# The shared expert of a mixture of experts computed behind the ninth expert unit instead of around the router

## The chip, the cores and the metric

One NeuronCore of a Trainium2 chip runs the whole program in one launch. The metric is device time in microseconds of one execution. Before the change three runs took 1607.09, 1607.56 and 1607.63 us; the median is 1607.56 us. A separate execution with the hardware profiler took 1610.33 us.

## The reference, cut to what matters

The program is two transformer blocks on 256 tokens of width 1024, all weights in fp32. The first block ends in a mixture of experts with 64 routed experts, 8 per token, and one shared expert that every token passes:

```python
def swiglu(x, wg, wu, wd):
    return (jax.nn.silu(x @ wg) * (x @ wu)) @ wd

h2 = modulate(rms_norm(x, norm_ffn_g), sh_ffn, sc_ffn)        # 256 x 1024
scores = jax.nn.sigmoid(h2 @ w_router)                        # 256 x 64
_, idx = lax.top_k(scores + b_router, 8)
wts = scores at idx, divided by their sum, times 2.5
routed[t] = sum over e in idx[t] of swiglu(h2[t], w_e_gate[e], w_e_up[e], w_e_down[e]) * wts[t, e]
y = swiglu(h2, w_sh_gate, w_sh_up, w_sh_down) + routed        # shared: 1024 -> 256 -> 1024
out = x + g_ffn * y
```

## The kernel before, in words

**Stages.** Most of the first block (input projection, attention, gating, output projection) runs until about 336 us of the profile. Then come the router (`routing`, called from `block1`), the mixture of experts (`moe`, until about 828 us) and the second block.

**Weights.** All weights are fetched by one stream of 1 MB transfers on SyncE's queue, in an order fixed when the kernel is built (`Ring`, line 222). During the experts there are 17 slots of 1 MB. `done` releases a slot and at once issues the next transfer of the list into it; SyncE works the list strictly in order. Each routed expert has three such chunks: two halves of gate and up, one of down. The shared expert has gate (`i_sh[0]`), up (`i_sh[1]`) and down (`i_sh[2]`). Before the change, gate and up stand in the list directly ahead of the first expert, and down behind unit 10 (`SH_DOWN`).

**Router stage.** For each half of the tokens (t = 0, 1) `x1_fm(t)` transposes the normalised tokens into `h2` (features in partitions), `logits(t)` multiplies them with the router's weights, `top(t)` selects eight on VectorE, `position()` counts with a few small matmuls, and `mkS(0)` builds the 0/1 matrix `S` that picks the tokens of the first units. The 32 matmuls of the shared expert's gate and up for t = 0 are put between these (`more`): one behind each router matmul, 4 behind the second transposes, 7 ahead of `position` and 5 behind it. `follow()` holds TensorE to that order.

**Experts.** The experts are taken in 26 units (`UNITS`) of one, two or four experts that share the 128 columns of the array, in 13 groups g of two units. For group g+1, `mkS` builds `S` and `gather` multiplies it with the normalised tokens (`xnh`, `xnl`, the high and low parts) to `xg`, 128 x 8 x 256, two quarters of it in each unit of group g. In unit p, `gu` multiplies `xg` with gate and up (in fp32, each expert in its own column group of the array), `act` applies silu and the product, `tra` transposes, `down` multiplies with the down weights, one unit late, and `comb` adds the rows into four accumulators, two units late. `trS` makes the matrix for `comb`.

The 32 shared matmuls for t = 1 are in unit 0, behind `trS` and ahead of its gathers; the shared down product (`shared_down`, 8 matmuls) is behind unit 10. Its result goes into the same accumulators.

**Order.** Source order is a priority only. When the kernel is built, a scheduler writes the order of each engine's instructions from the times at which it expects operands to be there. On the chip each engine runs its own list in order.

Of the kernel before, what the change touches and what calls it, by code (L numbers as in the profile page):

```python
# [9 lines left out]
F32 = mybir.dt.float32  # L10
F32R = mybir.dt.float32r
# [3 lines left out]
OP = mybir.AluOpType  # L15
# [256 lines left out]
class Kernel:  # L272
# [295 lines left out]
    def program(self):  # L568
        tc, nc, A = self.tc, self.nc, self.A
        with ExitStack() as es:  # L570
# [33 lines left out]
            for n in range(15, 33):  # L604
# [2 lines left out]
                self.i_ada += put([ada[j] for j in aorder[len(self.i_ada):len(self.i_ada) + na]], False)  # L607
            self.i_ga, self.i_gb, self.i_upa, self.i_upb, self.i_out = (
                ids[0:4], ids[4:8], ids[8:12], ids[12:14], ids[14:18])
            self.i_sh = put(w1[33:35], False)  # L610
            self.i_e, self.i_d = [], []
            self.of_rank = {}

            def chunk(r, j):
# [6 lines left out]
            for p, (n, r) in enumerate(UNITS):  # L621
                self.i_e.append(put([chunk(r + e, j) for j in range(2) for e in range(n)], False))
                if p:
                    self.i_d.append(downs(p - 1))
                if p == self.SH_DOWN:
                    self.i_sh += put(w1[35:36], False)
            self.i_d.append(downs(len(UNITS) - 1))
            self.i_2 = [put(w2[l * N_W2:(l + 1) * N_W2], True) for l in range(2)]
# [16 lines left out]
    R0 = 3  # L645
    HI = 2

    SH_DOWN = 10
    ADA_ORDER = (0, 1, 3, 4, 2, 5)
    ADA_AFTER = {8: 1, 10: 2, 11: 2, 12: 1, 13: 2, 14: 1, 15: 1, 16: 1, 17: 1, 18: 1, 19: 1, 20: 1, 21: 1}  # L650

# [130 lines left out]
    def block1(self):  # L782
# [353 lines left out]
        with self.follow():  # L1136
            x1_fm(0)
        x1_split(0)

        sh = iter(self.shared(h2, 0, self.mmp))  # L1140

        def more(n):
            for _ in range(n):
                next(sh)()

        for t in range(2):
            for f in logits(t):
                with self.follow():
                    f()
                    more(1)  # L1150
            if t == 0:
                with self.follow():
                    x1_fm(1)
                ends = [self.last(e) for e in (mybir.EngineType.Activation, mybir.EngineType.DVE)]
                with self.follow():
                    more(4)
        after = self.sigmoid
        with tc.issue_after(ends[0]), tc.issue_after(ends[1]):
            x1_split(1)
            top(0)  # L1160
        top(1)
        with self.follow():
            more(7)
        with self.follow():
            position()
        with self.follow():
            more(5)
        self.dump("h2", h2[:])
        adap_es.close()
        self.moe(xnh, xnl, gf, h2, after, mmes, ranks, overflow)  # L1170
        ext3_es.close()
        ext2_es.close()
        xp2_es.close()
# [355 lines left out]

        return pool.tile([128, 512], F32, tag="bank", name=name, bufs=3)  # L1530

    def shared(self, h2, t, pool):

        nc = self.nc
        ps = self.bank(pool, "shy") if t else pool.tile([128, 512], F32, tag="mm", name="shy")
        self.shp = ps

        def step(n, m, k):
            w = self.ring.get(self.i_sh[n])[:].rearrange("p (k c) -> p k c", k=8)
            j = 2 * n + m  # L1540
            nc.tensor.matmul(ps[:, j * 128:(j + 1) * 128], w[:, k, m * 128:(m + 1) * 128], h2[:, t, k],
                             start=j == 0 and k == 0, stop=j == 3 and k == 7, skip_group_check=True)
            if t and m and k == 7:
                self.ring.done(self.i_sh[n])

        return [lambda n=n, m=m, k=k: step(n, m, k) for n in range(2) for m in range(2) for k in range(8)]

    def shared_act(self, t):
        nc = self.nc
        if t == 0:  # L1550
            self.sgt = self.xp.tile([128, 2, 256], F32, tag="x01", name="sgt")
        ps = self.shp[:].rearrange("p (n m c) -> p n m c", n=2, m=2)
        o = self.sgt[:, :, t * 128:(t + 1) * 128]
        nc.scalar.activation(o, ps[:, 0], AF.Silu)
        nc.vector.tensor_tensor(o, o, ps[:, 1], op=OP.mult)

    def moe(self, xnh, xnl, gf, h2, after, mmes, ranks, overflow):
        tc, nc, A, c, sm = self.tc, self.nc, self.A, self.c, self.sm
        extp = self.extp
        mp, mp_es = self.pool("moe")  # L1560
# [4 lines left out]
        st = {}  # L1565
        nu = len(UNITS)
        xgs = [self.hip.tile([128, 8, 256], F32, tag="hl", name="xg")]
        wx = []
        for _ in range(2):
            t = self.hip.tile([128, SLOT], F32, tag="hl", name="wx")  # L1570
# [13 lines left out]
        def mkS(g):  # L1584
            S = mp.tile([128, 2, 2, 128], F32R, tag="S", name="S")
            for u in (2 * g, 2 * g + 1):
                n, _ = UNITS[u]
                for t in range(2):
                    i = nc.vector.tensor_tensor(unit(S, u)[:, t], io1[:, None, 0:128 // n].to_broadcast([128, n, 128 // n]),
                                                table(u, 0)[:, t], op=OP.is_equal)  # L1590
            st["S", g] = S
            return i

        def mkW(g):
            W = self.xp.tile([128, 2, 2, 128], F32, tag="x00", name="SW")
# [3 lines left out]

        def gather(g, q):  # L1600
            S = st["S", g]
            xg = xgs[g % 2]
            ps = self.bank(pg)
            for kk in range(2):
                k = 2 * q + kk
                o = ps[:, kk * 256:(kk + 1) * 256]
                n = 0
                for t in range(2):
                    for src in (xnh[:], xl):
                        nc.tensor.matmul(o, src[:, t, k * 128:(k + 1) * 128], S[:, t].rearrange("p u s -> p (u s)"),  # L1610
                                         start=kk == 0 and n == 0, stop=n == 3, skip_group_check=True)
                        n += 1
            for kk in range(2):
                k = 2 * q + kk
                i = ps[:, kk * 256:(kk + 1) * 256]
                if kk:
                    nc.vector.tensor_scalar(xg[:, k], i, self.a2[:, k:k + 1], self.mod[:, 3, k, 0:1], op0=OP.mult, op1=OP.add)
                else:
                    nc.scalar.activation(xg[:, k], i, AF.Identity, scale=self.a2[:, k:k + 1], bias=self.mod[:, 3, k, 0:1])

        def gu(p, k):
            if k == 0:
                st["gu"] = pg.tile([128, 512], F32, tag="gu", name="gu")
            xg = xgs[p // 2 % 2]
            n = UNITS[p][0]
            m = 128 // n
            ids = self.i_e[p][k // 4 * n:k // 4 * n + n]
            for e, i in enumerate(ids):
                s0 = (p % 2) * 128 + e * m
                w = self.ring.get(i)[:].rearrange("p (k c) -> p k c", k=4)  # L1630
                nc.tensor.matmul(st["gu"][m * e:m * e + m, :], xg[:, k, s0:s0 + m], w[:, k % 4, :], start=k == 0, stop=k == 7,  # L1631
                                 tile_position=(0, m * e))
            if k % 4 == 3:
                for i in ids:
                    self.ring.done(i)
# [41 lines left out]
        def comb(p):  # L1677
            ST = st.pop(("ST", p))[0]
            for h in range(2):
                yh, yl = st.pop(("y", p, h))  # L1680
                for t in range(2):
                    for y in (yh, yl):
                        nc.tensor.matmul(self.acc[t][h][:], ST[:, t * 128:(t + 1) * 128], y[:],
                                         start=False, stop=False, skip_group_check=True)

        def shared_down():
            i = self.i_sh[2]
            w = self.ring.get(i)[:].rearrange("p (k c) -> p k c", k=2)

            for k in range(2):  # L1690
                nc.vector.tensor_tensor(w[:, k], w[:, k], gf[:], op=OP.mult)
            for t in range(2):
                for h in range(2):
                    for k in range(2):
                        nc.tensor.matmul(self.acc[t][h][:], self.sgt[:, k, t * 128:(t + 1) * 128], w[:, k, h * 512:(h + 1) * 512],
                                         start=False, stop=False, skip_group_check=True)
            self.ring.done(i)

        i = mkS(0)
        ranks(None, -1)  # L1700
        with tc.issue_after(after.ins), tc.issue_after(i.ins):
            self.shared_act(0)
        mmes.close()
        pg = es.enter_context(tc.tile_pool(name="pg", bufs=1, space=PSUM))
        for q in range(5):
            if q < 4:
# [5 lines left out]
        for p in range(nu):  # L1712
            g = p // 2 + 1
            more = 2 * g < nu
            if p % 2 == 0 and more:
                mkS(g)

            for k in range(8):
                if p:
                    gu(p, k)  # L1720
                if k == 3:
                    if p > 1:
                        comb(p - 2)
                    trS(p)
                    if p == 0:
                        for f in self.shared(h2, 1, pg):
                            f()
                        self.shared_act(1)
                        xgs.append(self.hip.tile([128, 8, 256], F32, tag="hl", name="xg"))
                    if more:  # L1730
                        for q in range(2):
                            gather(g, 2 * (p % 2) + q)
                if p == 0 and k in (4, 7):
                    ranks(pg, int(k == 7))
            act(p)
            if p:
                down(p - 1, 0)
                down(p - 1, 1)
            tra(p)
            if p % 2 and more:  # L1740
                mkW(g)
            if p == 1:
                overflow(pg)
            if p == self.SH_DOWN:
                shared_down()
        self.fg = []
        for h in range(2):
# [657 lines left out]
```

## Time and profile before

| | |
|---|---|
| median of three runs | 1607.56 us |
| profiled execution | 1610.33 us, of which the span of the trace 1608.5 us |
| TensorE matmul (PE) busy | 1558.0 us (97%) |
| TensorE weight load (PEld) busy | 1204.3 us (75%) |
| VectorE / ScalarE busy | 874.2 us (54%) / 632.7 us (39%) |
| read from memory | 413.05 MB, 259 GB/s over the span |
| costliest group of the experts | L1631 `gu`, 936 records, 206.8 us |

Busy time of PE is the union of matmul records, whose ends are modelled. Each fp32 matmul leaves two records; some records are missing. The profile cuts the span in 40 slices of 40.2 us: the experts fill slices 10 to 21. L numbers are lines of the kernel before.

### The profile page before, as it was taken

What the parts mean: (1) busy time and instruction counts of PE and PEld (TensorE: products, weight loads), DVE (VectorE), ACT (ScalarE), POOL (GpSimd) and SP (SyncE); (2) the same over time, 40 slices, a digit from 0 to 9 for tenths busy, and PEclk for the clock granted to TensorE, in tenths of its full rate; (3) what the DMA queues carried; (4) which work ended last, traced back from release to release, by engine and by line L of the source; (5) the groups of instructions that cost most, each with busy time, mean ns of one, the idle gap of its engine ahead of it and who ended that gap; (6) DMA issues with size and microseconds to landing.
All of it is one profiled execution on the core that took longest, in us unless ns stands there. A gap on an engine that the chain in (4) does not pass through costs nothing. (4 is left out here: it accounts for less than half of the span.)

```text
span 1608.5 us, 26028 instructions
## 1 busy us (share of the span) xinstructions
PE 1558.0 (97%) x10509; PEld 1204.3 (75%) x10509; DVE 874.2 (54%) x1647; ACT 632.7 (39%) x1171; POOL 12.8 (1%) x23
## 2 busy tenths in 40 slices
PE   6999998999999999999989999999999999999997
PEld 4799876975444444444349999899999999899996
DVE  3696597663332323332354667864446566975454
ACT  3633376441111111111134656454433656544440
POOL 0000000000000000000000000000000000000000
PEclk9999899999999999999999999999999999999999
DMA  9789676879999999999965446565552444655530
GB/s 363 275 307 292 194 204 210 307 288 347 403 421 421 420 420 421 420 421 420 422 241 186 146 147 212 187 239 185 186 178 81 156 158 143 244 216 210 184 131 27
DMA packets 62973, 419.48 MB, mean 261 GB/s; under 512 B 7394, under 2 KB 9058, under 8 KB 14211
## 3 DMA queue, kind: packets, MB, share of 16 engines
q1 hardware_dynamic: 59010, 408.63, 67.6%
q0 software_dynamic: 1088, 5.61, 1.1%
q10 hardware_dynamic: 2752, 3.55, 0.6%
q8 instruction: 83, 1.36, 0.3%
q14 instruction: 40, 0.32, 0.1%
HBM read 413.05 MB, written 4.19 MB: 259 GB/s over the span
## 5 line engine op out<-in xcount | busy, mean ns | idle before, releaser
L353 DVE TENSOR_TENSOR wlo<-w,whi 128x1024 fp32r<-128x1024 f32 (+1 forms) x384 | 375.3, 1016 | 182.3 <-ACT whi L352 179.5
L352 ACT CAST whi<-w 128x1024 fp32r<-128x1024 f32 (+1 forms) x384 | 319.3, 883 | 317.2 <-PE mm L393 144.3
L392 PE MATMUL mm<-xTh,whi 128*128 128x256 f32 x960 | 274.5, 286 | 0.0
L394 PE MATMUL mm<-xTh,wlo 128*128 128x256 f32 x960 | 271.5, 283 | 0.0
L393 PE MATMUL mm<-xTl,whi 128*128 128x256 f32 x960 | 271.0, 282 | 0.0
L1631 PE MATMUL gu<-w,xg 128*64 128x512 f32 (+2 forms) x936 | 206.8, 596 | 0.0
L392 PEld LDWEIGHTS mm<-xTh,whi 128*128 128x128 f32 x960 | 182.9, 191 | 2.2 <-issue 1.4
L393 PEld LDWEIGHTS mm<-xTl,whi 128*128 128x128 f32 x960 | 183.4, 191 | 0.6
L394 PEld LDWEIGHTS mm<-xTh,wlo 128*128 128x128 f32 x960 | 182.8, 190 | 0.0
L1631 PEld LDWEIGHTS gu<-w,xg 128*64 128x64 f32 (+2 forms) x936 | 59.2, 127 | 99.4 <-issue 94.9
L1670 PE MATMUL y<-w,aT 128*64 128x512 f32 (+2 forms) x432 | 114.4, 599 | 0.0
L1768 ACT CAST yh<-yf 128x512 fp32r<-128x512 f32 x52 | 32.2, 619 | 126.1 <-DVE yf L1767 124.4
L1652 DVE SCALAR_TENSOR_TENSOR sil<-sil,wsl,gu 128x256 f32<-128x256 f32 x26 | 12.5, 481 | 126.6 <-ACT sil L1651 126.0
L1767 DVE TENSOR_TENSOR yf<-y,gf 128x512 f32<-128x512 f32 x52 | 35.9, 690 | 79.3 <-PE y L1670 79.3
L392 PE MATMUL mm<-hh,whi 128*128 128x256 f32 x256 | 74.4, 293 | 3.4 <-ACT whi L352 1.8
L394 PE MATMUL mm<-hh,wlo 128*128 128x256 f32 x256 | 74.9, 294 | 1.2 <-DVE wlo L353 1.0
L1670 PEld LDWEIGHTS y<-w,aT 128*64 128x64 f32 (+2 forms) x432 | 32.7, 126 | 57.5 <-issue 56.0
L393 PE MATMUL mm<-hl,whi 128*128 128x256 f32 x256 | 74.4, 292 | 0.5 <-DVE hl L289 0.5
L484 PE MATMUL acc<-whi,xTh 128*128 128x256 f32 x256 | 74.0, 290 | 0.0
L485 PE MATMUL acc<-wlo,xTh 128*128 128x256 f32 x256 | 72.8, 285 | 0.0
L486 PE MATMUL acc<-whi,xTl 128*128 128x256 f32 x256 | 72.6, 287 | 0.1
L1651 ACT ACTIVATE sil<-gu 128x256 f32<-128x256 f32 x26 | 10.0, 384 | 132.7 <-PE gu L1631 132.7
(450 smaller groups left out, 3119.3 us busy)
## 6 DMA issues: line engine op xcount, KB each, us to landing
w<-in_we SPq DMA_DIRECT2D x171, 1024.0 KB, 19.8
w<-in_w SPq DMA_DIRECT2D x156, 1024.0 KB, 4.9
w<-in_wada SPq DMA_DIRECT2D x23, 1024.0 KB, 9.8
wx<-in_we SPq DMA_DIRECT2D x21, 1024.0 KB, 19.8
ks<-kd SPq DMA_DIRECT2D x8, 512.0 KB, 8.1
lngb<-in_rows POOLq DMA_DIRECT2D x4, 1024.0 KB, 5.7
T<-in_rpb SPq DMA_DIRECT2D x8, 384.0 KB, 8.9
qs<-qd SPq DMA_DIRECT2D x16, 128.0 KB, 7.7
```

The costliest lines, as they stand in the source:

```text
L352: nc.scalar.copy(hi[:, s], w[:, s])
L353: self.lo_of[i] = nc.vector.tensor_tensor(lo[:, s], w[:, s], hi[:, s].bitcast(F32), op=OP.subtract)
L392: nc.tensor.matmul(ps, hi[:, k, mm], h, start=first, stop=False, skip_group_check=True)
L393: nc.tensor.matmul(ps, hi[:, k, mm], l, start=False, stop=False, skip_group_check=True)
L394: nc.tensor.matmul(ps, lo[:, k, mm], h, start=False, stop=last, skip_group_check=True)
L484: nc.tensor.matmul(o, h, wh, start=k == 0 and c % 2 == 0, stop=False, skip_group_check=True)
L485: nc.tensor.matmul(o, h, wl, start=False, stop=False, skip_group_check=True)
L486: nc.tensor.matmul(o, l, wh, start=False, stop=k == 7 and c % 2 == 1, skip_group_check=True)
L1631: nc.tensor.matmul(st["gu"][m * e:m * e + m, :], xg[:, k, s0:s0 + m], w[:, k % 4, :], start=k == 0, stop=k == 7, tile_position=(0, m * e))
L1670: nc.tensor.matmul(y[m * e:m * e + m, :], st["aT"][:, f * 128 + e * m:f * 128 + e * m + m], w[:, f, h * 512:(h + 1) * 512], start=f == 0, ...
L1767: nc.vector.tensor_tensor(t[0:n], y[0:n], g[0:n, h * 512:(h + 1) * 512], op=OP.mult)
L1768: nc.scalar.copy(yh[0:n], t[0:n])
```

## The change

Gate and up of the shared expert leave the head of the list of transfers and are put behind unit 9; shared down moves from behind unit 10 to behind unit 11. No shared matmul is left in the router stage or in unit 0. An extra group is put between groups 4 and 5: `mkI` builds an identity in place of `S`, and the usual `gather` with it, in units 8 and 9, gives `xg` for all 256 tokens. Group 5's own `mkS` and `gather` move from units 8 and 9 to behind unit 9, where each quarter of the gather follows one of four calls of `shared`, of 8 matmuls each, now 256 columns wide for both token halves at once. The second `xg` buffer is taken before the loop instead of inside unit 0.

```diff
-            self.i_sh = put(w1[33:35], False)
-                if p == self.SH_DOWN:
+                if p == self.P_SH:                    # P_SH = 9
+                    self.i_sh += put(w1[33:35], False)
+                if p == self.P_SH + 2:
                     self.i_sh += put(w1[35:36], False)
...
             for f in logits(t):
                 with self.follow():
                     f()
-                    more(1)
...
+        def mkI():
+            S = mp.tile([128, 2, 2, 128], F32R, tag="S", name="S")
+            for t in range(2):
+                o = S[:, t].rearrange("p u s -> p (u s)")
+                for h in range(2):
+                    i = o[:, h * 128:(h + 1) * 128]
+                    if h == t:
+                        nc.vector.tensor_copy(i, self.ident)
+                    else:
+                        nc.vector.tensor_scalar(i, self.ident, 0.0, None, op0=OP.mult)
...
+        def shared(n, m):
+            i = self.i_sh[n]
+            w = self.ring.get(i)[:].rearrange("p (k c) -> p k c", k=8)
+            if m == 0:
+                st["sh"] = self.bank(pg, "shy")
+            ps = st["sh"]
+            for k in range(8):
+                nc.tensor.matmul(ps[:, m * 256:(m + 1) * 256], w[:, k, m * 128:(m + 1) * 128], st["xg", "all"][:, k],
+                                 start=m == 0 and k == 0, stop=m == 1 and k == 7, skip_group_check=True)
+            if m:
+                f = sgt[:].rearrange("p a b -> p (a b)")
+                if n == 0:
+                    nc.scalar.activation(f, ps[:], AF.Silu)
+                else:
+                    nc.vector.tensor_tensor(f, f, ps[:], op=OP.mult)
+                self.ring.done(i)
...
             if p % 2 == 0 and more:
-                mkS(g)
+                mkI() if sh else mkS(g)               # sh: the group behind unit 9
...
-                    if p == 0:
-                        for f in self.shared(h2, 1, pg):
-                            f()
-                        self.shared_act(1)
...
             tra(p)
+            if p == self.P_SH:
+                mkS(g)
             if p % 2 and more:
                 mkW(g)
-            if p == self.SH_DOWN:
+            if p == self.P_SH:
+                for n in range(4):
+                    shared(n // 2, n % 2)
+                    gather(g, n)
+            if p == self.P_SH + 2:
                 shared_down()
```

## Rows read from the trace of the kernel before

**Rows 1.** Page, section 2: the span in 40 slices, DMA busy tenths and GB/s.
```profile
DMA  9789676879999999999965446565552444655530
GB/s 363 275 307 292 194 204 210 307 288 347 403 421 421 420 420 421 420 421 420 422 241 186 146 147 212 187 239 185 186 178 81 156 158 143 244 216 210 184 131 27
```

**Rows 2.** Busy time by stretch of 20 us: engines, granted clock, DMA share, GB/s.
```profile
360.00:380.00 20.00, 20.00 (x134) 13.48 (x133) 5.32 (x19) 3.57 (x9) 0.00 (x0) 1.00 0.83 316
380.00:400.00 20.00, 20.00 (x115) 10.36 (x116) 10.56 (x37) 4.68 (x11) 0.00 (x0) 1.00 0.94 349
400.00:420.00 20.00, 20.00 (x100) 8.69 (x98) 7.56 (x18) 3.56 (x8) 0.00 (x0) 1.00 0.98 392
```

**Rows 3.** SyncE queue's waits, first 380 to 440 us, then 500 to 560: total, times, longest.
```profile
SPq L222 <- PE gu L1631: 30.1, 7, 7.8
...
SPq L222 <- DMA w<-in_we: 37.7, 22, 2.0
```

**Rows 4.** Busy time by expert unit (4, 9, 20), columns as in rows 2.
```profile
421.30:436.60 15.30, 15.30 (x110) 6.77 (x108) 5.04 (x10) 3.18 (x7) 0.00 (x0) 1.00 1.01 416
...
511.20:530.20 19.00, 19.00 (x93) 8.18 (x93) 6.25 (x16) 3.14 (x7) 0.00 (x0) 1.00 1.01 420
...
711.00:732.30 21.30, 21.30 (x120) 8.91 (x119) 6.67 (x13) 3.85 (x8) 0.00 (x0) 1.00 1.01 421
```

**Rows 5.** Timeline of PE, down products behind gate and up of units 3 and 9: start, length.
```profile
417.45 3.60 PE L1670 MATMUL y<-w,aT 128*64 128x512 f32 x16
...
521.75 1.90 PE L1670 MATMUL y<-w,aT 128*32 128x512 f32 x4
523.59 0.44 PE L1658 MATMUL misc<-cst,sil 128*128 128x128 f32 x2
523.96 4.21 PE L1670 MATMUL y<-w,aT 128*32 128x512 f32 x28
```

**Rows 6.** Busy time by stretch of 2 us at the experts' end, columns as in rows 2.
```profile
820.00:822.00 2.00, 2.00 (x9) 0.60 (x12) 0.00 (x0) 0.00 (x0) 0.00 (x0) 1.00 0.63 262
822.00:824.00 2.00, 2.00 (x24) 0.76 (x19) 0.00 (x0) 0.00 (x0) 0.00 (x0) 1.00 0.09 37
```

**Rows 7.** Timeline of PE, router stage and unit 0; brackets: idle before, releaser.
```profile
348.23 0.33 PE L1400 MATMUL mm<-route,h 128*128 128x64 f32 x2
...
350.24 0.19 PE L1424 MATMUL mm<-mskb,ub 128*128 128x64 bf16 x1
...
352.73 0.39 PE L1610 MATMUL misc<-S,xnh 128*128 128x256 f32 x1 [0.93 <-DVE sgt L1555]
...
364.72 7.31 PE L1541 MATMUL shy<-h,w 128*128 128x128 f32 x64
371.79 0.36 PE L1610 MATMUL misc<-S,xnh 128*128 128x256 f32 x1
...
373.77 0.38 PE L1462 MATMUL misc<-cst,pw 128*128 128x128 f32 x2
```

**Rows 8.** Timeline of DVE in the router stage, columns as in rows 7.
```profile
344.47 1.79 DVE L1924 TENSOR_SCALAR h<-mm,a,mod 128x128 f32<-128x128 f32 x4 [1.24 <-ACT h L1927]
...
348.86 0.23 DVE L1409 TENSOR_TENSOR route<-route 128x64 f32<-128x64 f32 x1 [0.29 <-ACT route L1402]
...
352.12 0.15 DVE L1445 COPY cid<-mm 64x1 f32<-64x1 f32 x1
```

**Rows 9.** Shared down: records, ns min/median/max, first and last start us.
```profile
L1695 PE MATMUL acc<-wx,sgt x16: 592/592/697, 549.3 to 555.8; 128*128 128x512 f32 x16
```

**Rows 10.** Timeline of SyncE's queue: first transfers issued after the pause.
```profile
359.81 43.02 SPq L222 DMA_DIRECT2D w<-in_we  x15
```

**Rows 11.** A fall of PE's clock, stretches of 2 us, columns as in rows 2.
```profile
830.00:832.00 2.00, 0.00 (x0) 0.00 (x0) 1.79 (x13) 2.00 (x6) 0.00 (x0) 0.93 0.93 295
832.00:834.00 2.00, 1.27 (x6) 1.27 (x7) 2.00 (x5) 1.83 (x5) 0.00 (x0) 0.50 0.53 221
...
838.00:840.00 2.00, 2.00 (x16) 1.86 (x15) 2.00 (x5) 1.08 (x3) 0.00 (x0) 0.86 0.00 0
```

More of the change, by code (lines that the diff above doesn't have):

```diff
@@ L609, in program @@
                 ids[0:4], ids[4:8], ids[8:12], ids[12:14], ids[14:18])
-            self.i_sh = put(w1[33:35], False)
-            self.i_e, self.i_d = [], []
+            self.i_e, self.i_d, self.i_sh = [], [], []
             self.of_rank = {}
@@ L646 @@
     HI = 2
-    SH_DOWN = 10
+    P_SH = 9
     ADA_ORDER = (0, 1, 3, 4, 2, 5)
@@ L1138, in block1 @@
         x1_split(0)
[L1140 to L1144, printed above, removed]
         for t in range(2):
@@ L1154, in block1 @@
                 ends = [self.last(e) for e in (mybir.EngineType.Activation, mybir.EngineType.DVE)]
-                with self.follow():
-                    more(4)
-        after = self.sigmoid
         with tc.issue_after(ends[0]), tc.issue_after(ends[1]):
@@ L1162, in block1 @@
         with self.follow():
-            more(7)
-        with self.follow():
             position()
-        with self.follow():
-            more(5)
         self.dump("h2", h2[:])
         adap_es.close()
-        self.moe(xnh, xnl, gf, h2, after, mmes, ranks, overflow)
+        self.moe(xnh, xnl, gf, mmes, ranks, overflow)
         ext3_es.close()
@@ L1530, in bank, with moe @@
         return pool.tile([128, 512], F32, tag="bank", name=name, bufs=3)
[L1532 to L1557, printed above, removed]
+    def moe(self, xnh, xnl, gf, mmes, ranks, overflow):
         tc, nc, A, c, sm = self.tc, self.nc, self.A, self.c, self.sm
@@ L1567, in moe @@
         xgs = [self.hip.tile([128, 8, 256], F32, tag="hl", name="xg")]
+        gsh = self.P_SH // 2
         wx = []
@@ L1591, in mkS @@
             st["S", g] = S
+            st["xg", g] = xgs[(g + (g > gsh)) % 2]
             return i
+        def mkI():
[8 more added lines that the diff above has]
+                        nc.vector.tensor_scalar(i, self.ident, 0.0, None, op0=OP.mult)
+            st["S", "all"] = S
+            st["xg", "all"] = xgs[(gsh + 1) % 2]
         def mkW(g):
@@ L1601, in gather @@
             S = st["S", g]
-            xg = xgs[g % 2]
+            xg = st["xg", g]
             ps = self.bank(pg)
@@ L1623, in gu @@
                 st["gu"] = pg.tile([128, 512], F32, tag="gu", name="gu")
-            xg = xgs[p // 2 % 2]
+            xg = st["xg", p // 2]
             n = UNITS[p][0]
@@ L1684, in comb @@
                                          start=False, stop=False, skip_group_check=True)
+        sgt = self.xp.tile([128, 2, 256], F32, tag="x01", name="sgt")
+        def shared(n, m):
[14 more added lines that the diff above has]
+                self.ring.done(i)
         def shared_down():
@@ L1694, in shared_down @@
                     for k in range(2):
-                        nc.tensor.matmul(self.acc[t][h][:], self.sgt[:, k, t * 128:(t + 1) * 128], w[:, k, h * 512:(h + 1) * 512],
+                        nc.tensor.matmul(self.acc[t][h][:], sgt[:, k, t * 128:(t + 1) * 128], w[:, k, h * 512:(h + 1) * 512],
                                          start=False, stop=False, skip_group_check=True)
             self.ring.done(i)
-        i = mkS(0)
+        mkS(0)
         ranks(None, -1)
-        with tc.issue_after(after.ins), tc.issue_after(i.ins):
-            self.shared_act(0)
         mmes.close()
+        xgs.append(self.hip.tile([128, 8, 256], F32, tag="hl", name="xg"))
         pg = es.enter_context(tc.tile_pool(name="pg", bufs=1, space=PSUM))
@@ L1714, in moe @@
             more = 2 * g < nu
+            sh = g == gsh + 1
             if p % 2 == 0 and more:
-                mkS(g)
+                mkI() if sh else mkS(g)
             for k in range(8):
@@ L1724, in moe @@
                     trS(p)
-                    if p == 0:
-                        for f in self.shared(h2, 1, pg):
-                            f()
-                        self.shared_act(1)
-                        xgs.append(self.hip.tile([128, 8, 256], F32, tag="hl", name="xg"))
                     if more:
                         for q in range(2):
-                            gather(g, 2 * (p % 2) + q)
+                            gather("all" if sh else g, 2 * (p % 2) + q)
                 if p == 0 and k in (4, 7):
```

## The prediction, made before the changed kernel was run

> **What bounds the kernel now.** I read the page's slices first. From slice 11 to slice 19, which lies inside the experts, the DMA line stands at 9 and the rate at 420 to 422 GB/s [rows 1]; nowhere else is it so even. That rate is the ceiling of this stage: a chunk of 1 MB (1.049 million bytes at 421 GB/s) takes 2.49 us, and 192 routed chunks take 478 us. The stretches of 20 us show when the ceiling is reached: DMA share 0.83 from 360 us, 0.94 from 380, 0.98 from 400 [rows 2]. The waits of SyncE's queue say why. Between 380 and 440 us it waits for `gu` to give slots back (30.1 us); between 500 and 560 it waits for its own earlier transfers (37.7 us in 22 waits) and TensorE's releases have left the top of the list [rows 3]. So free slots are there and the stream is full.
>
> PE is shown busy all the time as well, and the two have to be told apart. Unit 4, with chunks in stock, took 15.3 us; unit 9 took 19.0 and unit 20 took 21.3, all with PE busy throughout [rows 4]. Every unit has about the same columns to multiply, so the longer units are not more work. The timeline shows what differs: behind unit 3 the two experts' down products leave 16 records in 3.60 us; behind unit 9 the scheduler took four records of one expert alone (1.90 us), then a transpose, then the other 28 in 4.21 us [rows 5]. Experts whose chunk is expected late are multiplied apart, and the column groups no longer run side by side. PE waits here in the form of a slower order. At the end the stream thins out between 820 and 822 us and is gone at 822 to 824, while the last down products run [rows 6]. The stage ends when the stream has ended, plus a few us.
>
> The Trainium skill bears on this reading (Trainium Kernel Development and Optimization, Performance Expectations): matmul busy time says little about how near TensorE is to its limit, and the share of time spent loading weights says more. The trace agrees: that share is 44% in unit 4 (6.77 of 15.3 us), 43% in unit 9 and 42% in unit 20, while busy time is full in all [rows 4]. By the page PE has room in the slow units; by busy time it has none, which is the first rival.
>
> **What goes away.** In unit 0 the 64 records of the shared product for t = 1 fill PE from 364.72 to the next gather at 371.79, 7.07 us [rows 7]. Nothing lies beside them: PE's list is in order, so all of that goes.
>
> In the router stage less goes, since there PE mostly waits. The first gather starts at 352.73 after 0.93 us of idling, released by VectorE's product for the shared expert (`sgt`), which frees the accumulator bank [rows 7]. Without it, the last reader of those banks is the count's copy, which ends at 352.27 [rows 8]: 0.46 us earlier. VectorE's own chain also waited 0.29 us for the second sigmoid [rows 8], which was late because the last router matmul sat among shared ones at 348.23 [rows 7], while the last part of `h2` was there at 346.26 [rows 8]. What VectorE does before and after fills its time, so I count 0.29 and not the 2 us: 0.7 us together. Ends: 0 if another reader holds the bank, 1.9 if the whole lateness of the matmuls is passed on. Sum of what goes from PE's path up to unit 1: 7.8 us (7.1 to 9.0).
>
> **What is added.** The identity gather is 32 matmuls of the size of any other; 16 of them took 371.79 to 373.77 [rows 7], so 4.0 us. The shared matmuls are half as many and twice as wide. A record of 128 columns cost 7.07/64 = 0.110 us [rows 7]; one of 512 columns, in shared down, (555.8 - 549.3)/15 = 0.433 us [rows 9]. Both scale with columns: 0.217 to 0.221 at 256, and 64 records make 13.9 us (at most 14.1). Net, PE's list grows by 17.9 - 7.8 = 10.1 us. `mkI`'s four VectorE instructions, eight more evictions and the shared silu and product lie beside PE, where VectorE is busy 6.25 and ScalarE 3.14 of 19.0 us [rows 4]. Uncovered, the wait for `mkS(5)` in front of its gather would cost about 1 us, but the first `shared` call lies ahead of it. Group 5's gather now ends right before unit 10 needs it; I allow 0.6 us, inside the rounding below.
>
> **What moves in the stream.** The number of transfers is the same. Gate and up gave two slots back in unit 0; after the change these two slots hold routed chunks from the start. From unit 1 on every release comes 7.8 us sooner, 3.1 transfers, of which two make up for the missing releases: 1.1 transfers net, 2.8 us. The other end is the idle share of the engines from 360 to 420 us, 20 x (0.17 + 0.06 + 0.02) = 5.0 us [rows 2], plus the 0.7 us by which the pause before 359.81 [rows 10] ends sooner: 5.7 us is all that the stream could win. I take 4.0 us, between the two, as neither is far off. Relative to the routed chunks PE loses nothing before unit 9: these stand two places further ahead in the list.
>
> Behind unit 9 PE is 10.1 us later than before and the stream 4 us earlier: chunks are in stock again, as in unit 4. The scheduler then has no reason to take experts apart, and the units run at 15.3 instead of 19.0 to 21.3 us [rows 4]: 3.7 to 6.0 us back per unit, so that 14.1 us are made up in three or four units, by about unit 14. From there both follow the stream. SyncE's queue doesn't starve meanwhile: it had free slots by then [rows 3]. Shared down moves one unit on, at the same cost. The second block sees only its start moved.
>
> So the end of the experts and of the program comes 4.0 us sooner. The profiled execution is the one summed: span 1608.5 to 1604.5, its time 1610.3 to 1606.3. The median of the runs lies 2.8 us below the profiled one; there it is 1607.56 - 4.0 = 1603.6 us.
>
> **Rivals.** First, on the slower side: PE's order stays slow. The 17.9 us of matmuls behind unit 9 are then paid in full, against 7.8 saved: +10.1 us, 1617.7. For it speaks that PE never idles in units 4, 9 and 20; against it that the same units cost 15.3 with stock and 21.3 without. The sign turns on one quantity: what the units behind the ninth win back. Under 10.1 us the change loses. If half of the 14.1 is won, the result is +3.1, 1610.7.
>
> Second, the clock. With the shared matmuls gone, PE in the router stage idles from about 346.6 (`h2` complete, last router matmul) to about 350, where `position` started at 350.24 [rows 7], and again until the gather. At the experts' end a stretch of idling was followed by half clock: a share of 0.93 means half speed in the last 0.28 us of its stretch, 0.86 in the first 0.56 us, so 831.7 to 838.6 us [rows 11], 6.9 us at 1.2 GHz, which can cost at most 3.4. A fall near 351 us would catch the gathers and the first `gu` from 352 to about 357.5 and cost 2.7 us. The gain shrinks to 1.3: 1606.3. The Trainium skill (TensorE: Matmul & The Clock Gate, Why this matters for your kernels) warns of idle gaps between bursts of matmuls, after which the clock is halved; the trace agrees at 832 us, and by that rule the sum is this rival's.
>
> Third, nothing comes of it: the last units keep the order they have, the head start of the stream ends in fuller slots, and the end stays: 1607.6.
>
> Fourth, more than forecast: units 5 to 9, with routed chunks two places ahead, also lose part of their slow order, one unit's 3.7 us: 1599.9.
>
> **How the numbers follow.** Forecast 0.42, slow order in full 0.10, half won back 0.14, clock 0.20, nothing 0.06, more 0.08. 0.2% is 3.2 us, about what a measurement here can tell from no change. Three quarters of the forecast's chance lie beyond it, all of the fourth rival, a little of the clock's: faster 0.44. Slower: the full slow order and most of the half, 0.22. The rest, 0.34, is within. The range runs from below the fourth rival, 1598, to 1615, which leaves out most of the full slow order; the forecast's own range is 1601.5 to 1606.
>
> **What would show it.** Right: no PE record of the shared product before unit 9, first gather near 352.0, unit 1 about 7.8 us sooner; DMA share near 1 by 410 us; 17 to 18 us between units 9 and 10 beyond a usual unit; units 10 to 14 near 15 to 16 us; last transfer about 4 us sooner. Wrong: units behind the ninth still at 19 us, SyncE waiting for `gu` for tens of us after unit 9, or a clock of 0.50 around 352 us.

## The result and the profile after

The changed kernel takes 1618.36 us (median of four runs, 1618.15 to 1619.26) beside 1607.38 us for the kernel before on the same chip: a recorded ratio of 1.0058, 95% interval 1.0043 to 1.0073, some 9 us slower; the two medians lie 11.0 us apart. The forecast was 1603.6 and the range ended at 1615; what came is the first rival, 1617.7. The profiled execution took 1618.28 us, its span 1616.1.

The slices of the page first, columns as in [rows 1]; PEclk is the granted clock in tenths of full speed.

```profile
PEclk9999999979999999999999999999999999999999
DMA  9789676869999999999945436565552444666530
GB/s 371 266 320 284 182 215 213 326 268 363 414 421 420 421 421 420 421 420 417 384 177 206 157 131 209 208 234 183 183 183 79 157 148 140 244 225 208 184 131 27
```

Two differences matter here. Slice 8, ahead of and in the router stage, lost clock: the kernel before has a 9 there. And slice 19, late in the experts, moved 384 GB/s where it was 422. The next rows show both closer, and the expert units; busy time by stretch of the kernel after, columns as in [rows 2].

```profile
336.00:338.00 2.00, 1.13 (x6) 0.89 (x6) 1.62 (x5) 2.00 (x7) 0.51 (x1) 1.00 1.01 426
338.00:340.00 2.00, 1.89 (x8) 1.70 (x8) 1.75 (x9) 1.07 (x4) 0.00 (x0) 0.54 0.97 356
...
350.00:352.00 2.00, 1.44 (x7) 1.47 (x8) 1.87 (x10) 0.00 (x0) 0.00 (x0) 0.50 0.02 8
...
354.00:356.00 2.00, 2.00 (x11) 1.43 (x12) 0.54 (x1) 0.56 (x1) 0.00 (x0) 0.69 0.00 0
...
503.30:538.70 35.40, 35.40 (x182) 23.20 (x181) 8.87 (x20) 5.42 (x11) 0.00 (x0) 1.00 1.01 420
538.70:553.40 14.70, 14.70 (x75) 6.74 (x75) 4.63 (x11) 3.13 (x7) 0.00 (x0) 1.00 1.01 421
553.40:583.10 29.70, 28.79 (x143) 12.66 (x142) 11.19 (x23) 4.93 (x10) 0.00 (x0) 1.00 1.01 420
...
719.10:740.30 21.20, 21.20 (x119) 8.85 (x118) 6.56 (x13) 3.84 (x8) 0.00 (x0) 1.00 1.00 413
...
820.00:822.00 2.00, 2.00 (x8) 0.57 (x8) 0.48 (x1) 0.21 (x1) 1.65 (x1) 1.00 1.01 422
822.00:824.00 2.00, 2.00 (x9) 0.70 (x10) 0.13 (x1) 0.00 (x0) 0.00 (x0) 1.00 0.28 115
```

The account by units needs a common start. The code ahead of the router is the same in both kernels, yet the router's first transposes (`x1_fm(0)`) start at 336.69 us of the profile before and at 334.25 of the one after. Over the nine profiled executions of this case that moment lies between 333.6 and 339.0 us, so the 2.4 us are not the change's doing. Where two kernels are compared, times are therefore counted from these transposes, unless they are called times of the profile or stand in its rows. The timelines of PE show them, and the start of unit 1's gate and up, columns as in [rows 7]; first the kernel before, then the changed one.

```profile
336.69 1.09 PE L1919 MATMUL mm<-cst,x 128*128 128x128 f32 x8 [0.38 <-DVE x L1108]
...
374.09 1.07 PE L1631 MATMUL gu<-w,xg 128*64 128x512 f32 x2
```

```profile
334.25 1.09 PE L1917 MATMUL mm<-cst,x 128*128 128x128 f32 x8 [0.38 <-DVE x L1109]
...
366.81 1.07 PE L1608 MATMUL gu<-w,xg 128*64 128x512 f32 x2
```

Unit 1's gate and up start 32.6 us behind the transposes (37.4 before), unit 9's 169.1 us (174.5): 5.4 us ahead. Unit 9 with the shared products lasts 35.4 us (19.0 before [rows 4]). Unit 10 then takes 14.7, as hoped, but unit 11, which now holds the 7 us of shared down, takes 29.7. In the kernel before units 10 and 11 had 26.1 (with shared down) and 19.1. So unit 12 starts 248.9 us behind the transposes instead of 238.7, 10.1 us later. From there nothing is made up: unit 20 takes 21.2 us (21.3 in [rows 4]), unit 25 starts at 476.3 instead of 465.8. From unit 12 to 25 both kernels take 17.5 us per unit (227.5 and 227.1 us over 13).

Why nothing is made up, the timelines of PE tell. Unit 21 of the kernel after:

```profile
740.32 1.07 PE L1608 MATMUL gu<-w,xg 128*64 128x512 f32 x2
...
743.86 7.08 PE L1608 MATMUL gu<-w,xg 128*64 128x512 f32 x30
750.87 1.90 PE L1647 MATMUL y<-w,aT 128*32 128x512 f32 x4
...
753.08 3.66 PE L1647 MATMUL y<-w,aT 128*32 128x512 f32 x28
```

And the same unit of the kernel before:

```profile
732.27 1.07 PE L1631 MATMUL gu<-w,xg 128*64 128x512 f32 x2
...
735.81 7.08 PE L1631 MATMUL gu<-w,xg 128*64 128x512 f32 x30
742.82 1.90 PE L1670 MATMUL y<-w,aT 128*32 128x512 f32 x4
...
745.02 3.66 PE L1670 MATMUL y<-w,aT 128*32 128x512 f32 x28
```

Record for record it is the same list, 8.05 us later in the profile, down to the four records of one expert that are multiplied alone in 1.90 us. From unit 13 on all of TensorE's records of the units come in the same order in both kernels. The order was written when the kernel was built; what lay in stock on the chip could not change it. And there was plenty: SyncE's queue in the kernel after, 680 to 740 and 740 to 800 us, shows what it waited for (total, times, longest).

```profile
SPq L222 <- PE gu L1608: 22.4, 7, 8.8
SPq L222 <- DMA w<-in_we: 12.7, 8, 2.2
...
SPq L222 <- PE y L1647: 2.0, 1, 2.0
...
SPq L222 <- PE gu L1608: 28.5, 8, 7.1
SPq L222 <- PE y L1647: 14.3, 4, 7.9
```

In the same stretches of the kernel before TensorE's `gu` held it for 2.2 and 6.5 us. After the change all slots are full, and the stream waits for TensorE.

The view that decides this, and that the prediction doesn't draw on, is PE's own waits. The kernel before, from 380 to 820 us, all that there are:

```profile
PE acc L1683 <- DVE yl L1769: 1.8, 3, 0.7
PE acc L1683 <- ACT yh L1768: 1.2, 5, 0.3
PE acc L1695 <- DVE wx L1691: 0.5, 1, 0.5
PE misc L1610 <- DVE yf L1767: 0.4, 1, 0.4
```

In 440 us PE did not wait once for a chunk of weights; in the changed kernel it did not either. Its list was what ended last, and the stream only stayed close ahead of it. It is close in unit 8, which took 18.4 us in the changed kernel: in three of the kernels below, with the same list up to there, PE waited for a chunk in it and the unit took 20.4 to 20.8 us. Work added to such a list is paid for, unless the rest of the list is written shorter. Here units 1 to 11 gave back 2.8 of the 17.7 us that were added behind unit 9, and the units behind them nothing.

### The profile page after: what moved, and what is told of

Same layout as the page of the kernel before. It is cut to its first block, busy times and chain, and to the rows that moved or that the text cites. A ratio compares the mean times of both kernels' runs of the same rounds, so it can differ in the third digit from the quotient of the medians.

```text
span 1616.1 us, 25978 instructions
## 1 busy us (share of the span) xinstructions
PE 1563.1 (97%) x10477; PEld 1209.7 (75%) x10477; DVE 876.4 (54%) x1654; ACT 634.5 (39%) x1174; POOL 12.8 (1%) x23
## 5 line engine op out<-in xcount | busy, mean ns | idle before, releaser
L1596 ACT ACTIVATE xg<-misc,mod,a 128x256 f32<-128x256 f32 x56 | 31.6, 563 | 79.7 <-PE misc L1587 79.7
```

## Experiments

**Does the order cost the time?** In both kernels TensorE's steps of the experts were held to source order: each step of `moe` runs in `follow()`, the helper that the router stage uses already, and `down` once for each f, so that the experts of a unit stay side by side.

```diff
+        def held(f):
+            def g(*args):
+                with self.follow():
+                    return f(*args)
+            return g
+
+        gather = held(gather)                 # and gu, trS, tra, comb, shared, shared_down
...
             for f in range(2):
-                for e in range(n):
+                with self.follow():
+                    for e in range(n):
```

Changed kernel, expected: 

> The changed kernel, same instructions, but the experts' TensorE steps (gather, gate and up per k, trS, comb, down per half, tra, shared) are held to source order, so that the experts of a unit are always multiplied side by side. Theory A (the scheduler's slow order is what is paid behind unit 9; TensorE is the bound and the added 10.1 us are paid because the order did not change): units with chunks in stock take 15 to 16 us, TensorE begins to wait for transfers, the stage then ends with the stream of weights, and the time is 1603 us (1600 to 1607), some 15 us under the changed kernel's 1618.4. Theory B (the transfers, or the slots, set the end in any order): 1616 to 1619 us, and the slow units stay at 18 to 21 us with TensorE idle in them instead of busy.

Kernel before, expected: 

> The kernel before, with the same steps held to source order. Theory A: TensorE needs 15 to 16 us per unit instead of up to 21, but here the stream of weights is full from 430 us on, so TensorE only changes slow order for waits: the end comes 0 to 3 us sooner, 1604.5 to 1607.5. Theory B: no change, 1607.4 within 1 us. If the slow order alone cost the 3 us per unit, the gain would be tens of us, and the stream would not have been full; that would be against both.

Measured: 1606.8 us for the changed kernel, ratio to the kernel before 0.9983 (0.9971 to 0.9994), and 1605.43 for the kernel before with held order, 0.9977 (0.9966 to 0.9987). (On this chip the kernel before gave 1609.0; the ratios count.) From unit 12 on most units now take 15 to 17 us and PE waits for weights, here in the changed kernel with held order, 380 to 820 us:

```profile
PE gu L1608 <- DMA w<-in_we: 7.6, 6, 1.5
PE y L1648 <- DMA w<-in_we: 7.1, 6, 2.2
...
```

Both end with the stream. The rows of the down products give the start of the last one, first for the changed kernel, then for the kernel before:

```profile
L1648 PE MATMUL y<-w,aT x424: 592/592/697, 378.6 to 820.2; 128*64 128x512 f32 x75, 128*32 128x512 f32 x63, 128*128 128x512 f32 x4
...
L1671 PE MATMUL y<-w,aT x432: 592/592/697, 384.0 to 820.8; 128*64 128x512 f32 x72, 128*32 128x512 f32 x66, 128*128 128x512 f32 x6
```

Their transposes start at 334.56 and 335.24 us, so the last down products come 485.6 us behind them in both. The order is thus worth 0.75% to the changed kernel (1.0058 against 0.9983) and 0.23% to the kernel before, and with it the change itself is worth nothing that can be told: the two intervals overlap. Both are faster than the kernel before as it stood.

**In which units?** The changed kernel was held to source order only from unit 10 on, and, as the counterpart, only in units 0 to 9. The diff is that above with a condition on the unit in hand.

```diff
             def g(*args):
+                if not st["now"] >= 10:               # counterpart: st["now"] < 10
+                    return f(*args)
                 with self.follow():
                     return f(*args)
```

Expected from unit 10 on: 

> The changed kernel with TensorE's steps of the experts held to source order only from unit 10 on; units 0 to 9 and the shared products behind unit 9 keep the scheduler's order. If the loss sits in the order behind the ninth unit: units 10 to 24 take 15 to 17 us instead of up to 21.5, unit 25 starts near 802 instead of 810.6 us, and the program takes 1605 to 1609 us. If the order of units 0 to 9 or the 10 us of work itself makes the loss: 1614 to 1619 us, and between them the shares of both are read.

Expected through unit 9: 

> The counterpart: source order in units 0 to 9 (with the shared products), the scheduler's order from unit 10 on. If the loss sits behind the ninth unit: 1616 to 1620 us, unit 25 again near 811 us. If the order of units 0 to 9 makes it: 1605 to 1609 us. If either half is enough to win it back (the stream binds again as soon as TensorE has room anywhere): 1606 to 1611 us here and in its counterpart too.

Measured: 1607.83 us from unit 10 on (ratio 0.9996, 0.9982 to 1.0010), 1621.86 through unit 9 (1.0077, 1.0054 to 1.0100). All of the loss sits behind the ninth unit. Units 20 and 23 with held order behind the ninth (unit 21 between them took 19.9 us, with 1.4 us of waiting for a chunk):

```profile
705.00:721.00 16.00, 16.00 (x110) 7.63 (x109) 5.17 (x10) 3.18 (x7) 0.00 (x0) 1.00 1.01 420
...
757.00:772.10 15.10, 15.10 (x77) 7.11 (x76) 5.63 (x12) 3.18 (x7) 0.00 (x0) 1.00 1.01 421
```

and units 20 and 21 of the counterpart:

```profile
726.30:747.60 21.30, 21.30 (x120) 8.93 (x119) 6.66 (x13) 3.85 (x8) 0.00 (x0) 1.00 0.95 381
747.60:766.20 18.60, 18.35 (x94) 7.57 (x93) 6.38 (x16) 3.13 (x7) 0.00 (x0) 1.00 1.01 422
```

With the order held behind the ninth, unit 25 starts at 785.8 us of the profile, 24.8 us sooner than in the changed kernel (24.4 counted from the transposes) and 16 us sooner than expected, and then waits for its chunks; that is where most of the head start ends. The counterpart is slower than expected, and shows the other side of the order. Held through the ninth, unit 8 sits 18.3 us in its gate and up (10.6 in the changed kernel), because there the chunks really are late. What the held order had saved in the units before is spent there: unit 9 starts 169.1 us behind the transposes in both. Unit 9 itself, where PE waits for chunks too, then takes 37.7 us instead of 35.4. Side by side wins where chunks are in stock, and wins nothing or loses where they are late.

**Why does the scheduler take them apart?** From unit 10 on the second half of each routed expert's gate and up isn't fetched; the first half's chunk stands in for it.

```diff
-                self.i_e.append(put([chunk(r + e, j) for j in range(2) for e in range(n)], False))
+                self.i_e.append(put([chunk(r + e, j) for j in range(2 if p < 10 else 1) for e in range(n)], False))
...
-            ids = self.i_e[p][k // 4 * n:k // 4 * n + n]
+            ids = self.i_e[p][k // 4 * n:k // 4 * n + n] if p < 10 else self.i_e[p]
...
-            if k % 4 == 3:
+            if k == 7 or k == 3 and p < 10:
```

Expected: 

> The changed kernel with the scheduler's order, but from unit 10 on the second half of each routed expert's gate and up isn't fetched: the first half's chunk stands in for both, so two transfers per expert instead of three and every matmul as before (the sums of these experts are not the reference's). Theory: the scheduler takes experts apart because by its own count of transfer times their chunks come late. Then it has no reason left, units 10 to 24 run at 15 to 16 us, and the program comes out at 1575 to 1590 us. Rival: the slow order comes from something else in its plan than the transfers (its cost of the instructions, the buffers): units keep 16 to 21 us and the program takes 1610 to 1618 us.

Measured: 1578.49 us in a single execution, the scheduler's own order. Units 12 and 20 of it:

```profile
576.80:592.00 15.20, 15.20 (x93) 6.98 (x93) 3.11 (x6) 2.56 (x6) 0.54 (x1) 1.00 0.99 404
...
697.80:713.10 15.30, 15.30 (x111) 6.80 (x110) 5.16 (x10) 3.18 (x7) 0.00 (x0) 1.00 0.55 213
```

With fewer transfers ahead of them, the same matmuls are written side by side and units 12 to 24 take 15.0 us on average. So it is the transfers, as the scheduler counts them, that set the experts apart. Fewer transfers also leave more slots free; whether the scheduler's time per transfer or its wait for a slot makes the chunks late was not separated. On the chip they weren't late: in the changed kernel the earliest recorded down chunk of each unit from 12 to 25 had landed 13 to 25 us before the unit's down products began (4 to 15 us in the kernel before; unit 13's landing isn't recorded). That the scheduler's count runs late against the chip is inferred from this; the times that it expected were not read.

**Does the size of the added work matter?** Of the 32 shared matmuls for gate and up only 4 were kept (the shared expert's sums lack the rest).

```diff
-            for k in range(8):
+            for k in range(1):
...
-                                 start=m == 0 and k == 0, stop=m == 1 and k == 7, skip_group_check=True)
+                                 start=m == 0, stop=m == 1, skip_group_check=True)
```

Expected: 

> The changed kernel with 4 of the 32 shared gate and up matmuls behind unit 9 (one k of eight in each call); the other 28 are left out. Theory A (TensorE is the bound, its list is paid instruction by instruction): 56 records of 0.217 us less, 12.2 us, so 1606.2 us (1605 to 1608). Theory B (the stream or the slots set the end): 1616 to 1619 us. If the scheduler answers to less work with a slower order behind unit 9, the gain is less than 12.2 us, by what units 10 and 11 lose.

Measured: 1613.67 us, ratio 1.0023 (1.0011 to 1.0035). The 12.2 us of the expectation did not come. Unit 9 fell from 35.4 to 24.6 us, yet from unit 9 to unit 12 only 3.0 of these 10.8 us were left (76.8 against 79.8): the scheduler stretched units 10 and 11 to 17.4 and 34.8 us, as it would if it expected its chunks no sooner. From unit 13 the order is once more that of both kernels. (Its profiled execution lies 3.1 us above its median; the unit lengths are read, not the end.)

**What did the clock cost?** 32 small matmuls of the identity were put where the shared ones had been in the router stage.

```diff
+        def more(n):                                  # n times nc.tensor.matmul(warm[...], self.ident, self.ident)
...
                 with self.follow():
                     f()
+                    more(1)
...
+                    more(4)                           # and more(7), more(5) around position()
```

Expected: 

> The changed kernel with 32 added matmuls of 128 x 128 by 128 columns in the router stage, of the identity with itself into a bank that nothing reads, at the places where the shared products stood before. Theory A with the clock: the granted clock stays at 1.00 from 350 to 360 us, the first gathers take 0.12 instead of 0.21 us each, unit 0 ends about 2 us sooner, and since TensorE is the bound to the end, the program does too: 1616.3 us. If the fall of the clock is hidden by the pause of the transfers or by a later wait: 1618.4 us.

Measured: 1618.19 us, ratio 1.0043 (1.0026 to 1.0060); the changed kernel's 1.0058 lies inside, so the time alone tells neither the 2.1 us of the expectation nor their absence. The timeline does. The clock stayed at 1.00 from 326 us to the end of the experts. Timeline of PE, this kernel:

```profile
337.25 1.09 PE L1934 MATMUL mm<-cst,x 128*128 128x128 f32 x8 [0.40 <-DVE x L1109]
...
352.96 0.36 PE L1604 MATMUL misc<-S,xnh 128*128 128x256 f32 x1 [0.61 <-DVE cid L1448]
353.16 0.28 PE L1604 MATMUL misc<-S,xnl 128*128 128x256 f32 x1
353.27 0.28 PE L1604 MATMUL misc<-S,xnh 128*128 128x256 f32 x1
...
367.14 1.07 PE L1625 MATMUL gu<-w,xg 128*64 128x512 f32 x2
...
494.44 3.62 PE L1625 MATMUL gu<-w,xg 128*32 128x512 f32 x26 [1.19 <-DMA w<-in_we]
```

and of the changed kernel, with the shared products of unit 9 below:

```profile
350.56 0.55 PE L1587 MATMUL misc<-S,xnh 128*128 128x256 f32 x1 [1.82 <-DVE cid L1431]
350.91 0.41 PE L1587 MATMUL misc<-S,xnl 128*128 128x256 f32 x1
351.13 0.41 PE L1587 MATMUL misc<-S,xnh 128*128 128x256 f32 x1
...
520.98 3.62 PE L1673 MATMUL shy<-xg,w 128*128 128x256 f32 x16
...
538.70 3.65 PE L1608 MATMUL gu<-w,xg 128*64 128x512 f32 x16
```

At 0.50 (1.2 GHz) the gathers follow one another at 0.21 us, at full clock at 0.12. From the first gather to unit 1 it is 16.2 us in the changed kernel (350.56 to 366.8) and 14.2 with the clock held (352.96 to 367.1): there the clock cost 2.1 us. The router stage, from the transposes to the first gather, took 16.3 us in the changed kernel, 15.7 with the filling work and 16.0 in the kernel before: it is shortest with the filling work. How long it would be at full clock without that work, no run shows. Together unit 1 starts 29.9 us behind the transposes instead of 32.6: 2.7 us won. Of these 2.2 are lost again in unit 8, which takes 20.7 us instead of 18.4 because its chunk is late (the wait of 1.19 us above). The last down products start 498.1 us behind the transposes instead of 498.5. Holding the clock so gained 0.4 us at the end, since unit 8 is where the stream still bound.

## Why the prediction was wrong

**The step that failed** is "The scheduler then has no reason to take experts apart, and the units run at 15.3 instead of 19.0 to 21.3 us [rows 4]: 3.7 to 6.0 us back per unit, so that 14.1 us are made up in three or four units". Chunks did come into stock behind unit 9, as said; the order did not answer to that stock. It was written before the run, and from unit 13 on it is the same list in both kernels. The held order from unit 10 on removes the loss (0.9996), fewer transfers remove the slow order itself (15.0 us per unit). The quantity named for the first rival, what the units behind the ninth win back, came out near nothing: unit 10 won 4.4 us once shared down is taken out of the unit before (26.1 - 7.0 - 14.7), and unit 11 gave 3.6 of it back (29.7 - 7.0 - 19.1).

**The reading behind it** was "The stage ends when the stream has ended, plus a few us." The stream ended at 822 us and the last down products at 825, but PE had not waited for it anywhere from 380 us on. It was called a wait "in the form of a slower order", and that holds only for an order that follows the stream. This one was fixed.

**Terms.** What is added was sized well: four groups of 16 records and a quarter of a gather each, from 520.98 to 538.70, 17.7 us, where 13.9 for the products plus the 4.0 of a gather had been counted. What goes was not: 4.8 us at unit 1 (37.4 - 32.6), for 7.8. Unit 0's 7.1 us went, but the half clock took 2.1 of them back, and the router stage took 16.3 us instead of 16.0, where 0.7 had been counted off. So the closeness to the first rival is in part luck: 3.0 us less were saved than its sum says, and units 1 to 11 gave back 2.8 that it doesn't have. The net is 10.1 us at unit 12 and 10.5 at unit 25, for the +10.1 summed and the 11.0 between the medians. The spans differ by only 7.6, since the profiled execution before came to the router 2.4 us later.

The stream's 4.0 us were a second step that failed, and a better order would not have brought them. By the prediction's own rule 4.8 us are 1.9 transfers, and two had to make up for the missing releases: nothing is left. In the first 320 us behind the transposes the engines moved at the same rate, here before and after:

```profile
336.69:656.69 320.00, 316.03 (x1700) 150.21 (x1701) 114.03 (x289) 64.34 (x145) 1.07 (x2) 1.00 0.97 395
```

```profile
334.25:654.25 320.00, 312.72 (x1620) 151.98 (x1620) 114.14 (x292) 64.43 (x143) 1.07 (x2) 0.97 0.96 395
```

And with held order, where the stream does end the stage, both kernels reach their last down products after the same 485.6 us. At the experts' end of the changed kernel the stream even runs later: 422 and 115 GB/s from 820 to 824 us where it was 262 and 37 [rows 6].

The second rival's fall of the clock came too, and earlier than placed: 0.54 at 338 to 340 us, after two stretches of 2 us in which PE was busy 1.53 and 1.13 us, then 0.50 until 355. It came in all six kernels that have no shared or filling matmuls in the router stage, and in none of the three that have them. It cost 2.7 us up to unit 1, as reckoned, and 0.4 at the end. The Trainium skill warns of idle gaps between bursts of matmuls (TensorE: Matmul & The Clock Gate, Why this matters for your kernels). That warning does not cover this fall: from 332 us to the fall no gap of PE was longer than 0.5 us.

The share of time spent loading weights did not tell the two cases apart. It is 42% in unit 20 of the changed kernel (8.85 of 21.2 us), where PE's list was the bound, and 48% (7.63 of 16.0) in the same unit with the order held behind the ninth, where the stream was. PE had room in the slow unit only if the order of its list changed. The Trainium skill names this share as a better measure than matmul busy time (Trainium Kernel Development and Optimization, Performance Expectations).

All three signs named for a wrong prediction were there: units at 19 us and more, SyncE waiting for `gu` for tens of us, and a clock of 0.50.

## What to carry to other kernels

When an engine is busy throughout a stage, look in that engine's waits for a wait on the stream: if there is none, take the engine's list for the bound, however full the stream looks, and expect to pay for work added to it. When the order of the list is written before the run, head start on the chip does not repair it; ask what the scheduler expects, or hold the order by hand where operands are known to be in stock. Before moving work to fill an engine elsewhere, check whether the present order already leaves time on the table: here holding the order alone gave 0.23% where moving the work lost 0.58%. And compare two profiles from a moment that the change can't have touched: here 2.4 us of the 7.9 by which unit 9 came sooner in the profile were there before the router.

## What the runs showed of the hardware

A full stream and a waiting queue can be had together. From 680 to 800 us of the changed kernel SyncE waited 50.9 us for `gu` and 16.3 for `y`, yet the slices at that time show 420 and 417 GB/s; only the last, with 384, shows the lack. Waits of the issuing queue alone do not prove that a stream starves.

With held order from unit 10 on, PE idled for a chunk at the very end and the clock fell there as well. Stretches of 2 us of that kernel:

```profile
816.00:818.00 2.00, 0.00 (x0) 0.00 (x0) 0.00 (x0) 0.00 (x0) 0.00 (x0) 1.00 1.01 410
818.00:820.00 2.00, 1.88 (x16) 0.64 (x20) 0.00 (x0) 0.00 (x0) 0.00 (x0) 0.85 0.93 381
820.00:822.00 2.00, 2.00 (x13) 0.40 (x5) 0.72 (x2) 0.62 (x1) 0.00 (x0) 0.50 0.68 283
```

That kernel's last down products start at 822.8 us, 488.9 us behind its transposes and 3.3 later than with the order held throughout, where the clock stayed at 1.00 in these stretches. How much of the 3.3 us is the clock's was not tried, and the intervals of the two ratios overlap.
